# The low part of every weight computed on VectorE in place of GpSimd, in a two-block fp32 model

## The chip, the cores and the metric

The kernel runs on one core of a Trainium2 chip. The metric is the device time of one execution in microseconds. The kernel before takes 2074.5 us, the median of three runs (2071.7, 2074.5, 2074.66).

## The reference

512 tokens of width 1024 go through two blocks in float32. Weights lie in DRAM, 175 MB of loads in all.

- Block 1: `x + rmsnorm(m @ w_out)`, where `m` joins a causal attention (8 heads, low-rank queries and keys of rank 256, rotary positions) and a short gated convolution; then a gated FFN, `(silu(h @ w_gate) * (h @ w_up)) @ w_down` with 2816 hidden features, and an embedding gate, `x + sigmoid(x @ w_ple_gate) * rmsnorm(p @ w_ple_proj)`.
- Block 2, two layers: retention (4 heads, keys of 256, values of 512, decays by chunk) with a squared-ReLU MLP of 4096, and a chunk attention (16 heads of 64, relative bias) with another such MLP; then a last RMS norm.

```python
def rmsnorm(x, g):
    xf = x.astype(jnp.float32)
    y = xf * lax.rsqrt(jnp.mean(xf * xf, axis=-1, keepdims=True) + EPS)
    return (y * g.astype(jnp.float32)).astype(x.dtype)

def _sqrelu_mlp(h, w1, w2):
    u = jax.nn.relu(h @ w1)
    return (u * u) @ w2
```

## The kernel before, in words

**Data and products.** Features lie on the partitions: `x0` to `x7` are eight tiles of 128 features x 512 tokens. Every float32 product is made of three float32r matmuls (`mm3`, L147 to L150). For that each operand is split in a first part, the value rounded to float32r, and a second part, what the rounding left. For activations the two parts are a `pair`: `split` (L113) and `split_gain` (L118; ScalarE at L120, VectorE at L121) make it. For the weights they are the tiles `wh` and `wl`.

**Weights.** `load_weights` (L132) takes one block of up to 128 x 1024 weights (512 KB): a load on SP's queue into `wr`, a copy on ScalarE that rounds it into `wh` (through the helper at L111), and the subtraction `wl = wr - wh` on GpSimd (L137). It is called 354 times; 298 of the blocks are 1024 wide. `wr`, `wh` and `wl` have three buffers each. The instructions are put 80 places ahead of where they are written (`HW`), so that a block is split some weights before TensorE needs it.

**Order.** TensorE's order is the program's own (L79): generators pause after each 128-row part, and products that are independent are pulled in between before each step that waits for another engine. The orders of VectorE, ScalarE, GpSimd and SP are made by a scheduler from the program's order and the priorities (`HW`, `HC`, `HT`).

**Steps around the change.** A norm's `Norm.column` (L236) sums by transposes on TensorE (L240); its `root` (L244 to L259) is a chain of twelve small VectorE operations, from a reduction (L247) to L259; `spread` (L262) hands the result back to TensorE (L265), which waits for it. The heads of the attentions make scores (L311 to L333), `turn` (L335) transposes the probabilities (L340) and splits them into two parts (`pt`: a copy on ScalarE through L111, a subtraction on VectorE through L108), and `pv` (L347, L355) multiplies by the values. The embedding gate's `embed_add` (L854) and `Next.take` (L866) add to `x`, split the new `x` for the next products and square it for the next norm. VectorE's small helpers are `mul` (L102), `add` (L105) and `sub` (L108), so that their instructions carry these lines whoever calls them.

**GpSimd's other work.** It issues the load of the gains (L453), a store of the rotary table to DRAM (L500) and eight loads from there (L504), and runs two multiplications near the end (L952).

Of the kernel before, what the change touches and what calls it, by code (L numbers as in the profile page):

```python
# [21 lines left out]
# How many instructions ahead of their place the weights', the norms' and the embedding's are taken up,  # L22
# and how many parts of the filling products run before each step that waits for another engine.
HW = 80  # the weights' parts
N_E = (19, 11)  # embedding's norm: before its column, before its rows
W_OUT = (8, 2, 2, 13, 13)  # the first boundary
DOWN = (12, 1, 3, 10, 12)  # the second boundary
HC = 100  # roots and rows of the norms
HE = 60  # the embedding's products
HT = 30  # turned probabilities  # L30
PER = (14, 10, 6)  # the last heads of the first attention
OUT = (6, 6)  # the attention's norm
LAT = (6, 6, 12, 6, 5, 8, 2)  # before the first attention
HID = (0, 9)  # FFN's norm
N_RET = (8, 5)  # retention's norm
N_MLP = ((9, 8), (9, 5))  # the MLPs' norms
N_CH = (14, 12)  # chunk attention's norm
GG = (6, 7, 6)  # a retention head's products and norm
FIN = (5, 8)  # the final norm
CO = (4, 11)  # the convolution's norm  # L40
PER2 = (10,) * 8 + (13, 10, 9) + (10,) * 5 + (3,)  # the heads of the chunk attention
# [19 lines left out]
def kernel(  # L61
# [7 lines left out]
    nc = tc.nc  # L69
# [11 lines left out]
    # ---------------------------------------------------------------- tiles and single steps  # L81
# [12 lines left out]
    def f32(ap):  # L94
        return ap.bitcast(F32)
# [17 lines left out]
    def split(dst, src, rows=slice(0, P)):  # L113
        """src as the sum of two float32r parts, exactly."""
        copy(dst[rows, 0, :], src[rows, :])
        sub(dst[rows, 1, :], src[rows, :], f32(dst[rows, 0, :]))
# [15 lines left out]
    def load_weights(t, src, c):  # L132
        raw, hi, lo = t
        sp.dma_start(raw[:, c], src[:, c])
        with tc.high_priority(offset=HW):
            copy(hi[:, c], raw[:, c])
            nc.gpsimd.tensor_tensor(out=lo[:, c], in0=raw[:, c], in1=f32(hi[:, c]), op=ALU.subtract)  # L137
# [14 lines left out]
    # Products come as generators that pause after each 128-row part, so that others run in between; after  # L152
    # the last part it is their caller that pauses, once what reads the product is in place.
# [23 lines left out]
    def units4(outs, src, acts, prepare=None, loaded=None, tok=ALL, pool=None):  # L177
        """Four products at once, in the order of the rows that they share."""
        loaded = [] if loaded is None else loaded
        for kk in range(KT // 2):  # L180
            if kk == len(loaded):
                loaded += load4(src, 1, acts, prepare, kk, pool if kk < 3 else None)
            w = loaded[kk]
            for k in range(2):
                a = acts[2 * kk + k]
                for m in range(4):
                    c = slice(k * T + m * P, k * T + (m + 1) * P)
                    mm3(outs[m][:, tok], w[0][:, c], w[1][:, c], a[:, 0, tok], a[:, 1, tok],
                        kk + k == 0, kk == KT // 2 - 1 and k == 1)
                    yield  # L190

    def units_tok(outs, src, r0, acts):
        """Products with the tokens on the partitions."""
        nk = len(acts)
        for kk in range(nk // 2):
            w = weights(src[(r0 + kk) * P:(r0 + kk + 1) * P, :])
            for t in range(NT):
                ts = slice(t * P, (t + 1) * P)
                for k in range(2):
                    a = acts[2 * kk + k]  # L200
                    c = slice(k * T, (k + 1) * T)
                    mm3(outs[t], a[:, 0, ts], a[:, 1, ts], w[0][:, c], w[1][:, c],
                        kk + k == 0, 2 * kk + k == nk - 1)
                    if 2 * kk + k < nk - 1 or t < NT - 1:
                        yield
# [11 lines left out]
    class Norm:  # L217
        """1/sqrt(mean of squares + eps) over the features: a column per token tile, and along the rows."""
# [25 lines left out]
        def root(self, ps):  # L244
            """A guess from the exponent, a Newton step with the constants that suit it, and a cubic step."""
            a, na, u, h, y, w = (small(dt=d, tag=g)[:, :self.nt] for d, g in ((F32, "sm"),) * 4 + ((I32, "smi"), (F32, "sm")))
            dve.tensor_reduce(out=a, in_=ps.rearrange("p (t f) -> p t f", f=P)[:, :self.nt, :], op=ALU.add, axis=AX.X)  # L247
            dve.tensor_scalar(a, a, 1.0 / self.n, EPS, ALU.mult, ALU.add)
            dve.tensor_scalar(y, a.bitcast(I32), -0.5, 1595932665.0, ALU.mult, ALU.add)
            dve.tensor_scalar(na, a, -0.703952253, None, ALU.mult)  # L250
            y = y.bitcast(F32)
            mul(u, y, y)
            mul(u, u, na)
            dve.scalar_tensor_tensor(out=y, in0=u, scalar=0.703952253 * 2.38924456, in1=y, op0=ALU.add, op1=ALU.mult)
            mul(u, y, y)
            mul(h, u, a)
            dve.tensor_scalar(w, y, 0.375, None, ALU.mult)
            dve.scalar_tensor_tensor(out=h, in0=h, scalar=-10.0 / 3.0, in1=h, op0=ALU.add, op1=ALU.mult)
            dve.scalar_tensor_tensor(out=w, in0=h, scalar=5.0, in1=w, op0=ALU.add, op1=ALU.mult)  # L259
            self.col = w  # L260
# [13 lines left out]
        def then(self, f):  # L274
            """Run f once the rows are there."""
# [11 lines left out]
    class SplitNorm:  # L287
        """The same in two halves of the tokens, so that the first is done while the second is computed."""
# [11 lines left out]
    class Head:  # L300
        """One head of softmax attention; q and k feature-major, v token-major."""
# [9 lines left out]
        def scores(self, i):  # L311
# [4 lines left out]
            if self.stacked:  # L316
                # q's two parts on the two halves of the rows, against the first part of k in both
# [6 lines left out]
            # minus the scaled scores, and their least per row, which is minus the maximum  # L324
# [22 lines left out]
        def pv(self):  # L347
            """Rows 0-63 and 64-127 of the result add up to the head's output."""
# [14 lines left out]
    def value_tile(pool, ps, col=None):  # L363
        """Values of eight heads, the two parts of each head side by side."""
# [15 lines left out]
    def attention(n, head, fill, per, ptp, last):  # L380
        """The heads in a software pipeline; parts of `fill` run in between on the tensor engine."""
# [24 lines left out]
    # ---------------------------------------------------------------- loads that everything needs  # L406
# [5 lines left out]
    # the table of the first activations is loaded while the data is on its way  # L412
# [5 lines left out]
    # per-layer embedding: its projection does not need x, and fills in while norms are on their way  # L418
# [24 lines left out]
    # ---------------------------------------------------------------- first block: mixer  # L443
    ys, ys_t, mixed = [], [], []
    n_post = SplitNorm(D)
    with tc.tile_pool(name="m1", bufs=1) as m1, tc.tile_pool(name="pt1", bufs=1) as ptp:
# [25 lines left out]
        # the rotary angles as turns, reduced exactly: 16 frequencies times 8 spans of 64 tokens  # L472
        trig = m1.tile([P, T], F32, name="trig", tag="trig")

        def angles():
# [25 lines left out]
            # cos in 32 rows, then -sin and sin in 16 rows each, twice  # L501
# [7 lines left out]
        # keys of an even and an odd head: 64 features of the head, 64 of the rotated part, in turned order  # L509
# [122 lines left out]
        def conv_out():  # L632
            """The convolution's part of the output projection, its norm applied to the products."""
# [61 lines left out]
        # the attention's part of the output projection, its norm applied to the products  # L695
# [15 lines left out]
        def att_out():  # L711
# [4 lines left out]
            # the last three tiles in halves of the tokens  # L716
# [17 lines left out]
    def post_norm_add(norm, ys, gname, nxt):  # L734
        """x plus the normed ys on the norm's tokens, and the next operand's parts, tile by tile."""
# [7 lines left out]
    def boundary(norm, ys, gname, nxt, fill, counts, src, acts, loaded):  # L743
        """From the last product of one step to the first four of the next, in halves of the tokens."""
# [16 lines left out]
    # ---------------------------------------------------------------- first block: FFN  # L761
# [98 lines left out]
    class Next:  # L860
        """Parts of x times the next pre-norm's gain, and its sum of squares."""
# [25 lines left out]
    # ---------------------------------------------------------------- the other block's MLP  # L887
# [40 lines left out]
    def finish(hid, ws):  # L928
        """The last three tiles in halves of the tokens, and the final norm of each half."""
# [44 lines left out]
    # ---------------------------------------------------------------- retention  # L974
    with tc.tile_pool(name="m2", bufs=1, reuse_waits="tile") as m2:
# [37 lines left out]
        def values(h):  # L1013
            """Token-major values, centred over the head's features: the outputs then have mean zero."""
# [101 lines left out]
    # ---------------------------------------------------------------- chunk attention  # L1116
# [93 lines left out]
def _constants():  # L1210
    """Arrays that depend on the shapes alone."""
# [115 lines left out]
```

## Time and profile before

| | us |
|---|---|
| median of three runs | 2074.5 |
| span of the profiled execution | 2072.2 |
| TensorE busy (matmuls) | 2001.0 |
| VectorE busy | 1121.0 |
| GpSimd busy | 821.0 |
| ScalarE busy | 804.2 |

The profiled execution has no time of its own beside its span; the median of the runs lies 2.3 us above that span. In the rows below PE is TensorE, DVE is VectorE, ACT is ScalarE, POOL is GpSimd. A busy time is a sum of the durations of an engine's instructions; it contains what an instruction stood still after it had begun.

### The profile page before, as it was taken

How to read it: one execution, taken by the hardware profiler on the slowest of the kernel's cores; microseconds unless marked ns; L12 is line 12 of the kernel's file. 1: busy time of each engine (PE TensorE's matmuls, PEld its weight loads, DVE VectorE, ACT ScalarE, POOL GpSimd, SP SyncE). 2: the span in 40 equal slices, each digit the busy share in tenths (PEclk: the TensorE clock that was granted, in tenths of full speed). 3: DMA queues.
4: the chain of work that ended last, by engine and by line, in shares of the span. 5: the costliest groups of instructions: out<-in, count | busy, mean ns of one | idle time of the engine just before them, and what ended most of it. 6: DMA issues, size and time to landing. Idle time of an engine off the chain costs nothing.

```text
span 2072.2 us, 23982 instructions
## 1 busy us (share of the span) xinstructions
PE 2001.0 (97%) x9340; PEld 1649.8 (80%) x9340; DVE 1121.0 (54%) x1813; ACT 804.2 (39%) x1298; POOL 821.0 (40%) x370
## 2 busy tenths in 40 slices
PE   7899799999998899999999999999999999999998
PEld 5777688888887688888878888888877777888887
DVE  7877883042348844605466253346587876243255
ACT  4577452232233443314433222223466653222222
POOL 5323424444452333343334444444322234444442
PEclk9999999999999999999999999999999999999999
DMA  4112213232332223232223323232222223232332
GB/s 165 59 62 73 96 56 100 93 101 93 99 97 94 72 77 97 82 100 74 82 92 92 102 92 102 92 102 91 97 82 68 64 78 101 92 102 92 102 92 71
DMA packets 58786, 185.32 MB, mean 89 GB/s; under 512 B 6784, under 2 KB 10000, under 8 KB 58672
## 3 DMA queue, kind: packets, MB, share of 16 engines
q1 hardware_dynamic: 53648, 175.76, 26.7%
q10 hardware_dynamic: 4688, 7.60, 1.3%
q8 instruction: 73, 1.20, 0.2%
q0 software_dynamic: 336, 0.42, 0.1%
q14 instruction: 41, 0.34, 0.1%
HBM read 181.56 MB, written 2.20 MB: 89 GB/s over the span
## 4 chain that ended last, share of the span: by engine, by line
PE 45%; issue 25%; POOL 16%; DVE 9%; ACT 3%; DMA 1%; POOLq 0%; SPq 0%; ACTq 0%; DVEq 0%
POOL wl L137 16%; PE bank L148 14%; PE bank L150 14%; PE bank L149 14%; DVE pair L108 1%; DVE tmp L102 1%; DVE small L102 1%; DVE tmp L105 1%; PE bank L355 1%; DVE x L105 1%; DVE pair L121 1%; PE bank L320 1%; DVE pair L105 0%; DVE pt L108 0%; DVE pair L126 0%
## 5 line engine op out<-in xcount | busy, mean ns | idle before, releaser
L137 POOL TENSOR_TENSOR wl<-wr,wh 128x1024 fp32r<-128x1024 f32 (+4 forms) x354 | 813.9, 2301 | 1213.5 <-ACT wh L111 1213.0
L148 PE MATMUL bank<-pair,wh 128*128 128x512 f32 (+1 forms) x2550 | 985.0, 386 | 11.8 <-ACT pair L120 8.1
L150 PE MATMUL bank<-pair,wh 128*128 128x512 f32 (+1 forms) x2550 | 972.9, 382 | 12.8 <-DVE pair L121 9.1
L149 PE MATMUL bank<-pair,wl 128*128 128x512 f32 (+1 forms) x2550 | 971.8, 381 | 1.9 <-POOL wl L137 1.9
L111 ACT ACTIVATE wh<-wr 128x1024 fp32r<-128x1024 f32 (+4 forms) x354 | 352.7, 998 | 888.1 <-PE bank L150 576.6
L150 PEld LDWEIGHTS bank<-pair,wh 128*128 128x128 f32 x2550 | 481.6, 189 | 110.7 <-DVE pair L121 13.9
L148 PEld LDWEIGHTS bank<-pair,wh 128*128 128x128 f32 x2550 | 481.8, 189 | 104.0 <-ACT pair L120 9.4
L149 PEld LDWEIGHTS bank<-pair,wl 128*128 128x128 f32 x2550 | 482.3, 189 | 89.2 <-POOL wl L137 3.2
L108 DVE TENSOR_TENSOR pair<-tmp,pair 128x512 fp32r<-128x512 f32 (+1 forms) x156 | 232.0, 1489 | 73.3 <-ACT pair L111 72.2
L102 DVE TENSOR_TENSOR tmp<-bank,rb 128x512 f32<-128x512 f32 (+1 forms) x140 | 94.4, 678 | 258.4 <-PE bank L150 249.8
L105 DVE TENSOR_TENSOR x<-x,bank 128x512 f32<-128x512 f32 (+1 forms) x99 | 66.3, 671 | 267.6 <-PE bank L150 267.5
L111 ACT ACTIVATE pair<-tmp 128x512 fp32r<-128x512 f32 (+1 forms) x188 | 118.4, 630 | 115.9 <-DVE tmp L1076 34.3
L105 DVE TENSOR_TENSOR tmp<-tmp 128x512 f32<-128x512 f32 (+1 forms) x107 | 90.9, 850 | 50.4 <-ACT tmp L233 48.7
L121 DVE SCALAR_TENSOR_TENSOR pair<-x,gn,pair 128x512 fp32r<-128x512 f32 (+1 forms) x56 | 69.8, 1248 | 25.6 <-ACT pair L120 25.5
L148 PE MATMUL bank<-wh,pair 128*128 128x512 f32 x200 | 79.7, 399 | 0.0
L150 PE MATMUL bank<-wl,pair 128*128 128x512 f32 x200 | 77.9, 390 | 0.0
L149 PE MATMUL bank<-wh,pair 128*128 128x512 f32 x200 | 77.9, 390 | 0.0
L327 ACT ACTIVATE tmp<-tmp,small 128x512 f32<-128x512 f32 (+1 forms) x96 | 53.2, 555 | 37.9 <-DVE small L325 35.5
L108 DVE TENSOR_TENSOR pt<-bank,pt 128x512 fp32r<-128x512 f32 (+1 forms) x96 | 42.9, 485 | 21.5 <-ACT pt L111 21.1
L120 ACT ACTIVATE pair<-x,gn 128x512 fp32r<-128x512 f32 (+1 forms) x56 | 36.5, 654 | 33.3 <-DVE x L105 32.8
L894 DVE SCALAR_TENSOR_TENSOR tmp<-tmp 128x512 f32<-128x512 f32 x64 | 46.8, 733 | 2.1
L111 ACT ACTIVATE pt<-bank 128x512 fp32r<-128x512 f32 (+1 forms) x96 | 38.0, 434 | 19.3 <-PE bank L340 17.8
(150 smaller groups left out, 1351.0 us busy)
## 6 DMA issues: line engine op xcount, KB each, us to landing
wr<-in_m_w_dram SPq DMA_DIRECT2D x128, 512.0 KB, 3.7
wr<-in_r_qkg_dram SPq DMA_DIRECT2D x32, 512.0 KB, 3.5
wr<-in_w_gate_dram SPq DMA_DIRECT2D x20, 512.0 KB, 3.4
wr<-in_w_up_dram SPq DMA_DIRECT2D x20, 512.0 KB, 3.4
wr<-in_w_down_dram SPq DMA_DIRECT2D x16, 512.0 KB, 3.5
wr<-in_r_v_dram SPq DMA_DIRECT2D x16, 512.0 KB, 3.4
wr<-in_r_out_dram SPq DMA_DIRECT2D x16, 512.0 KB, 3.7
wr<-in_a_qk_dram SPq DMA_DIRECT2D x16, 512.0 KB, 3.4
```

What stands on the lines that cost most here:

```text
L102: dve.tensor_tensor(out=out, in0=a, in1=b, op=ALU.mult)
L105: dve.tensor_tensor(out=out, in0=a, in1=b, op=ALU.add)
L108: dve.tensor_tensor(out=out, in0=a, in1=b, op=ALU.subtract)
L111: act.activation(out, a, AF.Copy)
L120: act.activation(dst[:, 0, tok], src[:, tok], AF.Copy, scale=gain)
L121: dve.scalar_tensor_tensor(out=dst[:, 1, tok], in0=src[:, tok], scalar=gain, in1=f32(dst[:, 0, tok]), op0=ALU.mult, op1=ALU.subtract)
L137: nc.gpsimd.tensor_tensor(out=lo[:, c], in0=raw[:, c], in1=f32(hi[:, c]), op=ALU.subtract)
L148: pe.matmul(out, lhsT=ah, rhs=bh, start=start, stop=False)
L149: pe.matmul(out, lhsT=al, rhs=bh, start=False, stop=False)
L150: pe.matmul(out, lhsT=ah, rhs=bl, start=False, stop=stop)
L327: act.activation(s[:, :n], s[:, :n], AF.Exp, bias=self.mx[:, col], scale=-1.0, accum_out=self.sm[:, col])
L894: dve.scalar_tensor_tensor(out=t, in0=t, scalar=0.0, in1=t, op0=ALU.max, op1=ALU.mult)
```

## The change

The subtraction that makes the low part of a block of weights is issued on VectorE, through the helper `sub`, in place of GpSimd. Its operands, its priority and the number of subtractions stay.

```diff
@@ -134,7 +134,7 @@
         sp.dma_start(raw[:, c], src[:, c])
         with tc.high_priority(offset=HW):
             copy(hi[:, c], raw[:, c])
-            nc.gpsimd.tensor_tensor(out=lo[:, c], in0=raw[:, c], in1=f32(hi[:, c]), op=ALU.subtract)
+            sub(lo[:, c], raw[:, c], f32(hi[:, c]))
```

The helper that it calls, in both kernels:

```python
    def sub(out, a, b):
        dve.tensor_tensor(out=out, in0=a, in1=b, op=ALU.subtract)
```

All other lines of the diff take out comments and doc strings. TensorE's and SP's orders are the same in both kernels. The 354 rows are gone from GpSimd's order, whose eight loads of L504 now follow each other, and stand in VectorE's, where the scheduler has put them as follows. ScalarE's `wh` copies have moved a little against its other work.

VectorE at the root of the attention's group norm, before (`att0` to `att3` are the attention's result, `small` the columns of the root, `wl` the low part of a weight):

```order
L247 TENSOR_REDUCE small_2010<-bank_2005 128x4
L121 SCALAR_TENSOR_TENSOR pair_2041<-att2_648,gn_77,pair_2041 128x512
L248 TENSOR_SCALAR small_2010<-small_2010 128x4
L102 TENSOR_TENSOR pair_1983<-bank_1998,rb_1894 128x512
L249 TENSOR_SCALAR small_2014<-small_2010 128x4
L250 TENSOR_SCALAR small_2011<-small_2010 128x4
L121 SCALAR_TENSOR_TENSOR pair_2044<-att3_649,gn_77,pair_2044 128x512
L102 TENSOR_TENSOR small_2012<-small_2014 128x4
L102 TENSOR_TENSOR small_2012<-small_2012,small_2011 128x4
L254 SCALAR_TENSOR_TENSOR small_2014<-small_2012,small_2014 128x4
```

The same place now, from the second small product on:

```order
L102 TENSOR_TENSOR small_2012<-small_2014 128x4
L108 TENSOR_TENSOR wl_2143<-wr_2141,wh_2142 128x1024
L102 TENSOR_TENSOR small_2012<-small_2012,small_2011 128x4
L108 TENSOR_TENSOR wl_2321<-wr_2319,wh_2320 128x512
L254 SCALAR_TENSOR_TENSOR small_2014<-small_2012,small_2014 128x4
L108 TENSOR_TENSOR wl_2321<-wr_2319,wh_2320 128x512
L102 TENSOR_TENSOR small_2012<-small_2014 128x4
```

Three weight rows now stand inside the root, which had none.

VectorE where the embedding gate ends and retention's norm begins, now (`x6` and `x7` are the last tiles of the activations, `tmp_5473` the sum of squares, `small_5711` the column of retention's root):

```order
L102 TENSOR_TENSOR tmp_5649<-tmp_5649,pair_5048 128x512
L121 SCALAR_TENSOR_TENSOR pair_5653<-x6_84,gn_77,pair_5653 128x512
L105 TENSOR_TENSOR x7_85<-x7_85,tmp_5649 128x512
L105 TENSOR_TENSOR tmp_5473<-tmp_5473,tmp_5656 128x512
L108 TENSOR_TENSOR wl_5786<-wr_5784,wh_5785 128x1024
L121 SCALAR_TENSOR_TENSOR pair_5659<-x7_85,gn_77,pair_5659 128x512
L105 TENSOR_TENSOR tmp_5473<-tmp_5473,tmp_5662 128x512
L247 TENSOR_REDUCE small_5711<-bank_5706 128x4
L108 TENSOR_TENSOR wl_5817<-wr_5815,wh_5816 128x1024
L248 TENSOR_SCALAR small_5711<-small_5711 128x4
```

Before, the same rows stood there without the two `wl`, and the addition to `x7` stood one place earlier, ahead of the split of `x6`.

VectorE in a head of the chunk attention, now (`pt` is the second part of the turned probabilities, `kl` the second part of a later head's keys):

```order
L1135 SCALAR_TENSOR_TENSOR tmp_11504<-bank_11414,rb_11134 128x512
L108 TENSOR_TENSOR wl_11729<-wr_11727,wh_11728 128x1024
L108 TENSOR_TENSOR pt_11528<-bank_11529,pt_11527 128x4x128
L108 TENSOR_TENSOR kl_11511<-tmp_11504,pair_11506 64x512
L108 TENSOR_TENSOR pt_11528<-bank_11539,pt_11527 128x3x128
L108 TENSOR_TENSOR pt_11528<-bank_11548,pt_11527 128x2x128
L108 TENSOR_TENSOR pt_11528<-bank_11553,pt_11527 128x128
```

A weight row stands right ahead of the first `pt` row; before, the two rows of `kl` stood before and after that row and no weight's.

## Rows read from the trace of the kernel before

**Rows 1.** The page, part 1: busy time, share of the span, instructions.

```profile
PE 2001.0 (97%) x9340; PEld 1649.8 (80%) x9340; DVE 1121.0 (54%) x1813; ACT 804.2 (39%) x1298; POOL 821.0 (40%) x370
```

**Rows 2.** Waits of TensorE: what it waited for, us in total, times, longest.

```profile
PE bank L265 <- DVE small L259: 25.1, 8, 6.5
PE bank L150 <- DVE pair L121: 9.1, 6, 2.6
PE bank L148 <- ACT pair L120: 8.1, 4, 6.2
PE bank L355 <- DVE pt L108: 4.7, 5, 2.2
...
PE bank L150 <- DVE pair L108: 3.7, 2, 1.9
...
PE bank L149 <- POOL wl L137: 1.9, 3, 1.3
```

**Rows 3.** Busy time by stretch: length, then engine by engine, clock, DMA share, GB/s.

```profile
41.00:51.00 10.00, 3.51 (x13) 2.81 (x12) 7.99 (x11) 1.23 (x2) 6.25 (x7) 0.66 0.40 120
...
310.00:600.00 290.00, 290.00 (x1280) 239.90 (x1279) 82.85 (x83) 81.72 (x100) 129.95 (x55) 1.00 0.30 95
...
665.00:712.00 47.00, 40.76 (x166) 31.36 (x165) 43.51 (x57) 19.78 (x30) 17.79 (x7) 0.89 0.23 76
...
1480.00:1680.00 200.00, 200.00 (x928) 150.67 (x927) 157.60 (x393) 128.77 (x286) 51.68 (x25) 1.00 0.23 71
```

**Rows 4.** Groups of instructions by form: busy us, mean ns, idle before them.

```profile
L137 POOL TENSOR_TENSOR wl<-wr,wh 128x1024 fp32r<-128x1024 f32 x298 | 728.7, 2446 | 1089.1 <-ACT wh L111 1088.9
...
L108 DVE TENSOR_TENSOR pair<-tmp,pair 128x512 fp32r<-128x512 f32 x140 | 213.1, 1524 | 70.3 <-ACT pair L111 69.6
...
L121 DVE SCALAR_TENSOR_TENSOR pair<-x,gn,pair 128x512 fp32r<-128x512 f32 x40 | 62.2, 1556 | 25.5 <-ACT pair L120 25.5
```

**Rows 5.** Timeline of VectorE, the embedding gate's end: start and duration, us.

```profile
677.33 0.69 DVE L102 TENSOR_TENSOR tmp<-tmp,pair 128x512 f32<-128x512 f32 x1
678.05 2.78 DVE L105 TENSOR_TENSOR x<-x,tmp 128x512 f32<-128x512 f32 x1
```

**Rows 6.** Timeline of GpSimd, the same stretch.

```profile
677.45 2.83 POOL L137 TENSOR_TENSOR wl<-wr,wh 128x1024 fp32r<-128x1024 f32 x1 [6.76 <-ACT wh L111]
```

**Rows 7.** The page, part 5: all subtractions of the weights.

```profile
L137 POOL TENSOR_TENSOR wl<-wr,wh 128x1024 fp32r<-128x1024 f32 (+4 forms) x354 | 813.9, 2301 | 1213.5 <-ACT wh L111 1213.0
```

**Rows 8.** Timeline of VectorE at a root beside which GpSimd is idle.

```profile
655.88 0.43 DVE L108 TENSOR_TENSOR pair<-x,pair 128x256 fp32r<-128x256 f32 x1 [0.48 <-ACT pair L111]
656.56 0.69 DVE L247 TENSOR_REDUCE small<-bank 128x4 f32<-128x512 f32 x1 [0.25 <-PE bank L240]
...
658.88 0.16 DVE L259 SCALAR_TENSOR_TENSOR small<-small 128x4 f32<-128x4 f32 x1
```

**Rows 9.** Timeline of VectorE at the first norm's root.

```profile
36.56 0.69 DVE L247 TENSOR_REDUCE small<-bank 128x4 f32<-128x512 f32 x1 [2.01 <-PE bank L240]
...
38.65 3.91 DVE L102 TENSOR_TENSOR small<-small 128x4 f32<-128x4 f32 x2
...
42.79 4.49 DVE L102 TENSOR_TENSOR small<-small 128x4 f32<-128x4 f32 x2
...
47.52 0.16 DVE L259 SCALAR_TENSOR_TENSOR small<-small 128x4 f32<-128x4 f32 x1
```

**Rows 10.** Timeline of GpSimd at the first norm's root.

```profile
38.34 1.61 POOL L504 DMA_DIRECT2D trig<-hbm  x3
39.96 2.38 POOL L137 TENSOR_TENSOR wl<-wr,wh 128x1024 fp32r<-128x1024 f32 x1
42.28 2.62 POOL L504 DMA_DIRECT2D trig<-hbm  x5
44.90 2.35 POOL L137 TENSOR_TENSOR wl<-wr,wh 128x1024 fp32r<-128x1024 f32 x1
```

**Rows 11.** Tile `pt` from 1480 to 1690 us: who waited for it (us, times).

```profile
  DVE pt L108: 16.2, 21
```

## The prediction

> **What bounds the kernel now.** I read the busy times first. TensorE is busy for 97% of the span, VectorE for 54%, GpSimd for 40% [rows 1]. The sum of the products is not touched, so the change can only reach the 71 us in which TensorE stands still, and the stretches in which it runs at its lower clock level.
>
> The second view is the list of what TensorE waits for [rows 2]. VectorE ends most of these waits: 25.1 us behind the roots of the norms (eight waits, the longest 6.5), then 9.1 and 3.7 us behind the second parts of activations (`pair`), 4.7 us behind turned probabilities (`pt`). ScalarE's 8.1 us are 6.2 us at the very start, where the first input is on its way, and 1.9 us of the same splits. GpSimd itself, which makes the second parts of the weights (`wl`), is waited for only three times, 1.9 us together. So the price of GpSimd is not its lateness.
>
> The third view, busy times by stretch [rows 3], says where there is nothing to gain: in the FFN (310 to 600 us) TensorE is busy for 290.00 of 290 us and in the chunk attention (1480 to 1680) for 200.00 of 200. It also shows the clock: a mean grant of 0.66 from 41 to 51 us and 0.89 from 665 to 712 us. [...]
>
> What GpSimd does cost is in the durations of VectorE. The `pair` subtraction over 512 columns takes 1.52 us in the mean of 140, the scaled split 1.56 us in the mean of 40 [rows 4]. An undisturbed row of 512 takes 0.69 us [rows 5]. The next row, which starts at 678.05, takes 2.78 us [rows 5], while GpSimd runs a `wl` from 677.45 for 2.83 us [rows 6]: VectorE is held until GpSimd is done, 2.09 us longer than its own work. [...]
>
> **The change part by part.** *Removed*: 354 GpSimd subtractions, 813.9 us [rows 7]; 298 of them are 1024 wide at 2.45 us [rows 4]. With them go the holds.
>
> *Added*: the same 354 on VectorE. No two-input row of 1024 stands in the trace. 512 columns take 0.69 us [rows 5], 256 take 0.43 us [rows 8], so 256 more cost 0.26 and 1024 cost 0.69 + 2 x 0.26 = 1.21 us; the upper end is two rows of 512, 1.38. I take 1.21. Scaled from GpSimd's total (1.21/2.446 = 0.495) that is 403 us for all. The two groups of [rows 4] give back 140 x (1.52 - 0.69) + 40 x (1.56 - 0.69) = 151 us, and other forms were held too. VectorE ends at 1121 + 403 - 151 = 1373 us or less, at most 66%. A hold of 2.09 us thus becomes 1.21 us in the queue where a `wl` stands in the same place (-0.88, 42%), and nothing where it stands elsewhere.
>
> *The first norm's root.* Alone the root takes from 656.56 to 659.04, 2.48 us [rows 8]. At the start it runs from 36.56 to 47.68 [rows 9], with two pairs of tiny products lasting 3.91 and 4.49 us while GpSimd subtracts at 39.96 and 44.90 and issues table loads at 38.34 and 42.28 [rows 10]. TensorE stands still for it for 6.5 us [rows 2], so from about 41.2. The new order has one `wl` ahead of the root and none in it: it would end near 39.0, or 40.3 behind that `wl`, before TensorE is there. But the eight table loads (1.61 + 2.62 us) stay on GpSimd, now in one row. The product at 38.65 stood still for 1.3 us before the subtraction of 39.96 began, under those loads. If all eight hold, the root ends near 43.2 and 2.0 us of the wait are left; if none does, 0. I take 1.5 left, nearer to the row that was held: **-5.0**. [...]
>
> *The clock behind it.* 10 us at 0.66 are 3.4 us lost. With the idle time mostly gone I take half back: **-1.7**. The 47 x 0.11 = 5.2 us of the other stretch I leave, as TensorE will still stand still there.
>
> *The other roots.* 25.1 - 6.5 = 18.6 us in seven waits. The last one comes after the last weight and stays; the one in the second boundary keeps three `wl` rows in its way. The other five lose 0.88 each: **-4.4**. In the attention's norm the new order puts a whole and two half `wl` into the root, against the holds of before.
>
> *Splits.* 9.1 + 3.7 + 1.9 = 14.7 us. The chain before retention is typical: VectorE is busy for 43.5 of 47 us there [rows 3], and the holds are all that makes it late; the new order has a `wl` between most of its splits. Between 42% (each hold replaced on the spot) and 100% I take two thirds: **-9.8**.
>
> *Turned probabilities.* Of 4.7 us a quarter: **-1.2**.
>
> *Costs.* In both attentions a `wl` now stands just ahead of `pt` subtractions, right ahead of the first in ten of the 16 chunk heads. What covers it: VectorE waited there anyway for ScalarE's copy, 16.2 us in 21 waits [rows 11], 0.77 each; 1.21 - 0.77 = 0.44 is uncovered. For 16 heads that is 7.0 us at most, for ten 4.4; TensorE had no wait there and so some reserve: **+3.0** (0 to 7.0). For the first attention's eight heads 3.5 at most, I take half: **+1.7**. Without any cover each `wl` costs its 1.21.
>
> *Steady products: 0.* From 310 to 600 us, 55 `wl` add 55 x 1.21 = 67 us to VectorE's 83 of 290 [rows 3], so it is half idle still; a `wl` is made two weights ahead. TensorE's order and the loads' order don't change.
>
> Sum: -5.0 - 1.7 - 4.4 - 9.8 - 1.2 + 3.0 + 1.7 = -17.4 us on a span of 2072.2, so 2054.8. The median of the runs, 2074.5, is 2.3 above that span; I predict 2074.5 - 17.4 = **2057.1 us**, with 2047 to 2067 for this case.
>
> **The rivals.**
> *Given back.* Each `wl` lands in VectorE's queue in the very place where its hold was, and waits there for ScalarE's first part (`wh`), with all that stands behind it. For it: the order's many `wl` rows between splits. Against it: 2.09 against 1.21 us. Result 2070 to 2079, likeliest 2074.5.
>
> *Slower: VectorE too full in the attentions.* Each of 24 heads has a `wl` ahead of its `pt` row or its softmax. From 1480 to 1680 us VectorE is already busy for 157.6 of 200 us; 51.68 x 0.495 = 26 us of `wl` make up to 184, 92% [rows 3]. If no idle time covers them and TensorE waits the full 1.21 per head, that is +29.0 in place of the two costs above, against -22.1 of gains: +6.9, **2081.4 us**. It decides from 22.1/24 = 0.92 us per head. Against it: part of the 157.6 is holds that go. [...]
>
> *Larger gain.* All of these waits go (25.1 + 9.1 + 4.7 + 3.7 + 1.9 = 44.5) and both low stretches of the clock (8.6): 2074.5 - 53.1 = 2021.4. Against it: a root's own 2.48 us and ScalarE's rows remain.
>
> *Not what it says.* GpSimd's subtractions remain: the new order has none of them, so 1 in 100, 2074.5.
>
> **How the numbers follow.** The forecast has 0.58, the larger gain 0.05, given back 0.14, slower 0.22, not what it says 0.01. With 0.2% of 2074.5, 4.1 us, as about what a measurement can tell from no change, faster has 0.58 + 0.05 = 0.63, same 0.15, slower 0.22. The range: downward the forecast with the first root free (-1.5), all of the splits (-4.9), all of the clock (-6.9) and no costs (-4.7), 2057.1 - 18.0 = 2039; upward to the slower rival, 2081. About half of that rival's chance and most of the larger gain's lie outside.
>
> **What would show it.** GpSimd's busy time falls below 15 us; `wl` rows on VectorE take 1.2 us; `pair` subtractions fall to 0.7 us and the scaled split to 0.75; VectorE's busy time lies between 1200 and 1373 us; TensorE's wait at 41 us falls to 2 us or less; the chunk attention shows at most 0.2 us of new waits per head. I am wrong if TensorE waits for `wl` on VectorE by more than 10 us in all, if new waits of `pt` over 1 us per head appear between 1480 and 1680 us, if the stretch from 310 to 600 us is no longer full, or if the wait at 41 us stays with GpSimd free of subtractions.

## The result and the profile after

The changed kernel takes 2029.2 us (median of four runs, 2028.2 to 2030.7) against 2074.6: the ratio is 0.9776, with a 95% interval of 0.9762 to 0.979, so 45 us faster. The forecast was 17.4 us faster, 2057.1 us; the direction was right, and the size 2.6 times too small. The time lies below the range of 2047 to 2067, and below the 2039 to which the prediction's best cases add up. The span went from 2072.2 to 2028.9 us, by 43.3. Three executions of the later experiments ran in a slow state (2209.6 us at `HW` 60, 2837.3 at `HW` 100, 4999.9 of the kernel before beside them) and are left out of the medians below.

The page of the changed kernel, part 1, against [rows 1]:

```profile
PE 1991.5 (98%) x9340; PEld 1647.9 (81%) x9340; DVE 1197.2 (59%) x2167; ACT 805.5 (40%) x1298; POOL 7.1 (0%) x16
```

TensorE runs the same 9340 matmuls in 9.5 us less. VectorE took over 354 rows, 405.7 us of work, and is busy for only 76 us more: its other rows got some 330 us shorter.

What TensorE waits for now (us in total, times, longest), against [rows 2]:

```profile
PE bank L148 <- ACT pair L120: 9.5, 4, 6.1
PE bank L265 <- DVE small L259: 9.1, 6, 2.3
PE bank L340 <- ACT tmp L331: 4.5, 4, 2.5
PE bank L240 <- DVE tmp L105: 4.1, 3, 2.3
PE bank L150 <- DVE pair L121: 1.5, 3, 0.9
PE bank L355 <- ACT pt L111: 0.9, 1, 0.9
PE bank L355 <- DVE pt L108: 0.8, 1, 0.8
PE bank L148 <- ACT tmp L111: 0.3, 1, 0.3
```

The waits for the roots fell from 25.1 to 9.1 us. Those for VectorE's splits (L150) fell from 12.8 to 1.5, while those for ScalarE's splits (L120) rose from 1.9 to 3.4 beside the 6.1 of the start. No matmul waits for a weight's low part. All idle time of TensorE between matmuls adds up to 64.9 us before and 30.8 after.

The groups by form (busy us, mean ns, idle before them), against [rows 4]:

```profile
L108 DVE TENSOR_TENSOR wl<-wr,wh 128x1024 fp32r<-128x1024 f32 x298 | 364.1, 1222 | 144.6 <-ACT wh L111 143.7
...
L108 DVE TENSOR_TENSOR pair<-tmp,pair 128x512 fp32r<-128x512 f32 x140 | 95.7, 686 | 11.2 <-ACT pair L111 10.8
...
L121 DVE SCALAR_TENSOR_TENSOR pair<-x,gn,pair 128x512 fp32r<-128x512 f32 x40 | 29.8, 745 | 1.9 <-ACT pair L120 1.7
```

A weight's row takes 1.22 us on VectorE where GpSimd needed 2.45. The `pair` subtraction is back from 1524 to 686 ns, the scaled split from 1556 to 745.

The first norm's root, VectorE's timeline, against [rows 9]:

```profile
36.80 0.36 DVE L102 TENSOR_TENSOR small<-small 128x4 f32<-128x4 f32 x2
37.20 0.16 DVE L254 SCALAR_TENSOR_TENSOR small<-small 128x4 f32<-128x4 f32 x1
37.39 0.36 DVE L102 TENSOR_TENSOR small<-small 128x4 f32<-128x4 f32 x2
...
37.98 0.16 DVE L259 SCALAR_TENSOR_TENSOR small<-small 128x4 f32<-128x4 f32 x1
```

And GpSimd's timeline beside it, against [rows 10]:

```profile
37.21 4.21 POOL L504 DMA_DIRECT2D trig<-hbm  x8 [2.46 <-DMA hbm<-sc]
```

The second pair of products runs in 0.36 us in the middle of the eight table loads, where a pair took 3.91 and 4.49 before. The root is done at 38.1 us, and TensorE does not wait for it at all.

The trace of the kernel before already had the two products of its second pair apart, in narrower windows of VectorE's timeline:

```profile
42.79 0.16 DVE L102 TENSOR_TENSOR small<-small 128x4 f32<-128x4 f32 x1
```

```profile
42.99 4.29 DVE L102 TENSOR_TENSOR small<-small 128x4 f32<-128x4 f32 x1
```

The first of them ran free under the five table loads of [rows 10] (42.28 to 44.90 us). The second ended at 47.28 us, when the subtraction beside it ended (47.25).

Two stretches, the FFN and the chunk attention, at their new times (length, then PE, PEld, DVE, ACT, POOL, clock, DMA share, GB/s), against [rows 3]:

```profile
282.00:572.00 290.00, 290.00 (x1281) 240.11 (x1281) 118.57 (x138) 81.77 (x100) 0.00 (x0) 1.00 0.30 95
...
1439.00:1639.00 200.00, 200.00 (x928) 150.70 (x927) 159.65 (x417) 128.53 (x286) 0.00 (x0) 1.00 0.22 69
```

Both stay full. In the chunk attention VectorE has 24 rows more than before and is busy for 159.65 in place of 157.60 us: the holds that went paid for the weights' rows that came.

**Where the time came from.** TensorE's order is the same in every kernel here, so the start of one and the same matmul can be compared between two traces. The table gives how much earlier (-) or later a matmul starts than in the kernel before, at places named by their time there; each number is the difference of two start times. The columns after the first are the experiments below. Each column is one execution; that of e4_twice was 5.8 us slower than the median of its runs, the others lie within 3.1 us of theirs.

| place, us | changed | e1_both | e5_memset | e3_waits | e3_steady | e4_twice | e6_first |
|---|---|---|---|---|---|---|---|
| 47.8 | -8.3 | +1.8 | -8.4 | -8.3 | +0.2 | -7.4 | -9.6 |
| 310 | -27.7 | +34.3 | -26.0 | -27.6 | +0.5 | -1.2 | -10.6 |
| 600 | -28.0 | +34.0 | -26.2 | -27.9 | +0.5 | -1.5 | -10.6 |
| 712 | -37.8 | +49.4 | -38.7 | -39.9 | +0.3 | -0.2 | -10.5 |
| 1045 | -37.9 | +50.3 | -38.7 | -39.9 | +0.3 | -0.2 | -10.5 |
| 1062 | -41.3 | +53.6 | -42.2 | -43.4 | -1.3 | -2.0 | -10.5 |
| 1480 | -41.4 | +53.7 | -42.3 | -43.4 | -1.4 | -2.0 | -10.5 |
| 1680 | -41.4 | +58.4 | -42.3 | -43.5 | -1.4 | +8.4 | -10.5 |
| 1720 | -43.1 | +65.9 | -44.9 | -45.2 | -1.6 | +12.1 | -10.4 |
| end | -43.3 | +65.6 | -45.1 | -45.1 | -2.0 | +11.3 | -10.5 |

The first column moves in four places only: up to 310 us (27.7 of the 43.3), and at the boundaries near 650, 1050 and 1700 us. From 310 to 600, 712 to 1045, 1062 to 1680 and 1720 on it moves by 0.3 us or less.

### The profile page after: what moved, and what is told of

Its sections match the earlier page's. It is cut to its first block, busy times and chain, and to the rows that moved or that the text cites. A ratio compares the mean times of both kernels' runs of the same rounds, so it can differ in the third digit from the quotient of the medians.

```text
span 2028.9 us, 23868 instructions
## 1 busy us (share of the span) xinstructions
PE 1991.5 (98%) x9340; PEld 1647.9 (81%) x9340; DVE 1197.2 (59%) x2167; ACT 805.5 (40%) x1298; POOL 7.1 (0%) x16
## 4 chain that ended last, share of the span: by engine, by line
PE 90%; DVE 5%; ACT 3%; issue 1%; DMA 0%; POOL 0%; POOLq 0%; DVEq 0%; ACTq 0%
PE bank L148 29%; PE bank L150 28%; PE bank L149 28%; PE bank L355 1%; DVE wl L108 1%; PE bank L320 1%; PE bank L340 1%; PE bank L319 1%; DVE tmp L105 1%; DVE pair L108 1%; ACT tmp L327 1%; ACT wh L111 1%; PE bank L265 0%; DVE pair L121 0%; DVE x L105 0%
## 5 line engine op out<-in xcount | busy, mean ns | idle before, releaser
L148 PE MATMUL bank<-pair,wh 128*128 128x512 f32 (+1 forms) x2550 | 983.3, 386 | 9.5 <-ACT pair L120 9.5
L150 PE MATMUL bank<-pair,wh 128*128 128x512 f32 (+1 forms) x2550 | 971.9, 381 | 1.7 <-DVE pair L121 1.5
L148 PEld LDWEIGHTS bank<-pair,wh 128*128 128x128 f32 x2550 | 481.6, 189 | 101.2 <-ACT pair L120 10.8
L150 PEld LDWEIGHTS bank<-pair,wh 128*128 128x128 f32 x2550 | 481.3, 189 | 96.8 <-DVE pair L121 3.8
L108 DVE TENSOR_TENSOR wl<-wr,wh 128x1024 fp32r<-128x1024 f32 (+4 forms) x354 | 405.5, 1146 | 153.6 <-ACT wh L111 152.3
L108 DVE TENSOR_TENSOR pair<-tmp,pair 128x512 fp32r<-128x512 f32 (+1 forms) x156 | 106.7, 686 | 11.7 <-ACT pair L111 10.8
L105 DVE TENSOR_TENSOR tmp<-tmp 128x512 f32<-128x512 f32 (+1 forms) x107 | 68.1, 640 | 36.7 <-ACT tmp L233 36.0
L148 PE MATMUL bank<-wh,pair 128*128 128x512 f32 x200 | 79.7, 398 | 0.3 <-ACT tmp L111 0.3
L150 PE MATMUL bank<-wl,pair 128*128 128x512 f32 x200 | 78.0, 390 | 0.0
L108 DVE TENSOR_TENSOR pt<-bank,pt 128x512 fp32r<-128x512 f32 (+1 forms) x96 | 43.5, 486 | 15.5 <-ACT pt L111 15.1
L148 PEld LDWEIGHTS bank<-wh,pair 128*128 128x128 f32 x200 | 37.6, 188 | 8.6 <-ACT tmp L111 0.7
L150 PEld LDWEIGHTS bank<-wl,pair 128*128 128x128 f32 x200 | 37.5, 188 | 8.0
```

Source lines behind the costliest of these rows:

```text
L105: dve.tensor_tensor(out=out, in0=a, in1=b, op=ALU.add)
L108: dve.tensor_tensor(out=out, in0=a, in1=b, op=ALU.subtract)
L148: pe.matmul(out, lhsT=ah, rhs=bh, start=start, stop=False)
L150: pe.matmul(out, lhsT=ah, rhs=bl, start=False, stop=stop)
```

## The experiments

Two theories stood against each other. *Hold*: rows of VectorE no longer stand still while GpSimd reads. *Lateness or order*: the low part is ready sooner, or the scheduler's new orders are better. All times are medians of three to ten executions in three rounds, against the kernel before on the same chip (whose medians were 2074.5 to 2076.2 us).

**e1_both and e5_memset: is it GpSimd's reading?** Both keep VectorE's subtraction; GpSimd then writes over the raw weight, once with a subtraction, once with zeros. The two kernels have the same orders on all other engines; only GpSimd's instruction differs. Against the changed kernel, 18 places in VectorE's order and 4 in ScalarE's differ. The computed low parts are unchanged. In the code below, against the changed kernel, `sub(...)` stands for the call that is kept.

```diff
-            sub(lo[:, c], raw[:, c], f32(hi[:, c]))
+            sub(...); nc.gpsimd.tensor_tensor(out=raw[:, c], in0=raw[:, c], in1=f32(hi[:, c]), op=ALU.subtract)   # e1
+            sub(...); nc.gpsimd.memset(raw[:, c], 0.0)   # e5
```

> VectorE makes every low part as in the changed kernel, and GpSimd then subtracts over the same block once more, in place in the raw weight, whose value nobody reads. Theory 'hold' (the gain came from rows of VectorE no longer standing still while GpSimd reads): the holds are back on top of the queue's 405 us, the pair subtraction over 512 columns has a mean over 1.2 us, VectorE is busy for over 1400 us, and the time is 2060 to 2110 us. Theory 'lateness or order' (the gain came from the low part being ready sooner, 1.22 in place of 2.45 us, or from the scheduler's new orders): both are kept, so 2029 us, within 8.

> As e1_both with the same orders, but GpSimd fills the raw weight with zeros after use in place of the subtraction, so that it writes SBUF and reads nothing. Theory 'hold, reads only' (a row of VectorE with two SBUF inputs stands still only against a GpSimd instruction that reads): the pair subtraction stays at 0.69 to 0.75 us in the mean, and the time is within 6 us of 2029; only one-input rows of VectorE could be held. Theory 'hold, any GpSimd instruction': the pair subtraction is over 0.9 us, and the time is above 2040 us.

e1_both takes 2136.4 us (ratio 1.0289, 1.0271 to 1.0307), above the 2060 to 2110 that "hold" gave, and e5_memset 2029.9 us (0.9775, 0.976 to 0.979). In e1_both, waits and groups:

```profile
PE bank L265 <- DVE small L259: 37.6, 10, 9.0
...
PE bank L149 <- DVE wl L108: 2.8, 4, 1.3
```

```profile
L137 POOL TENSOR_TENSOR wr<-wr,wh 128x1024 f32<-128x1024 f32 x298 | 771.8, 2590 | 1110.9 <-DVE wl L108 983.1 <-ACT tmp L327 31.2 <-issue 23.6
...
L108 DVE TENSOR_TENSOR pair<-tmp,pair 128x512 fp32r<-128x512 f32 x140 | 114.4, 819 | 11.7 <-ACT pair L111 10.8
```

The roots' waits are back and larger, though VectorE makes the low part: by the traces it is done 1.26 us behind its `wh` in the median, as in the changed kernel, where GpSimd needed 2.47 before. TensorE waits for it only 2.8 us. So lateness is not the cause. (Part 4 of the page before puts 16% of the chain that ended last on GpSimd's subtractions. TensorE waited 1.9 us for them, so that share is no price either.) The `pair` mean is 0.82 us and not over 1.2 as expected: GpSimd's copy of the work now starts behind VectorE's (983.1 of its 1110.9 us of idle time end there) and meets other rows, by the waits the roots above all. In e5_memset, groups by form:

```profile
L137 POOL MEMSET wr<- 128x1024 f32 x298 | 284.9, 956 | 1512.7 <-DVE wl L108 1399.6 <-DVE small L329 38.2 <-DVE small L102 19.5
L108 DVE TENSOR_TENSOR pair<-tmp,pair 128x512 fp32r<-128x512 f32 x140 | 95.9, 686 | 11.2 <-ACT pair L111 10.8
```

354 GpSimd instructions that only write cost nothing that the time shows, and rows with two SBUF inputs keep their 686 ns. That a fill is shorter than a subtraction is not the reason: by the trace 89 of these 140 rows ran beside a fill, and none took over 694 ns. One-input rows are another matter. The same line in e5_memset and then in the changed kernel (a one-input operation of the root; ns as least, median and longest):

```profile
L249 DVE TENSOR_SCALAR small<-small x21: 159/170/970, 36.5 to 2018.3; 128x4 int32<-128x4 int32 x15, 128x2 int32<-128x2 int32 x6
```

```profile
L249 DVE TENSOR_SCALAR small<-small x21: 156/169/172, 36.6 to 2020.1; 128x4 int32<-128x4 int32 x15, 128x2 int32<-128x2 int32 x6
```

Four of them took 333 to 970 ns, each beside a fill, in place of 172 at most. So in these runs GpSimd's subtractions, which read, held the two-input rows (`pair` 1524 ns in the mean before, 819 in e1_both) and its fills, which only write, did not (686); some one-input rows were held by both (L249 2378 ns at most in e1_both, 970 in e5_memset). Why the two kinds of row differ, the profile does not show.

**e3_waits and e3_steady: which weights matter?** The low parts of 116 blocks around the waits go to VectorE and the other 238 to GpSimd, and the other way round. The line takes the place of the `sub` of the changed kernel; dots stand for arguments.

```diff
+            NL.append(1); n = len(NL) - 1; (sub(...)) if any(n in r for r in (range(54), range(98, 130), range(176, 185), range(280, 297), range(350, 354))) else nc.gpsimd.tensor_tensor(...)   # e3_waits; e3_steady: not any(...)
```

> VectorE makes the low parts of 116 blocks (the first 54, and 32, 9, 17 and 4 around the later boundaries), GpSimd those of the 238 blocks that are split in the steady stretches and the chunk attention. Theory 'hold, and only where TensorE waits': the whole gain is kept, 2026 to 2034 us, with VectorE's pair subtraction still slow in the steady stretches. Theory 'relief over the whole span': a gain in proportion to the blocks, 45 x 116/354 = 15, so 2060 us.

> The other way round: VectorE makes the 238 low parts of the steady stretches, GpSimd the 116 around the boundaries. Theory 'hold, and only where TensorE waits': no gain, 2068 to 2078 us. Theory 'relief over the whole span': 45 x 238/354 = 30 us less, 2044 us.

e3_waits takes 2029.1 us (0.9772, 0.9757 to 0.9787), e3_steady 2074.3 us (0.9991, 0.998 to 1.0003). A third of the blocks carries the whole gain, the other two thirds none. e3_waits, groups by form:

```profile
L137 POOL TENSOR_TENSOR wl<-wr,wh 128x1024 fp32r<-128x1024 f32 x232 | 566.6, 2442 | 1325.2 <-ACT wh L111 1325.2
L108 DVE TENSOR_TENSOR pair<-tmp,pair 128x512 fp32r<-128x512 f32 x140 | 207.0, 1480 | 64.5 <-ACT pair L111 64.0
```

The `pair` subtraction is as slow as before, 1480 ns, and the time is that of the changed kernel. The row on which I priced the hold, in its mean over the span, is mostly from places where a hold is free.

**e6_first: the first norm's root alone.** Only the first 12 blocks go to VectorE (`if n < 12`).

> Only the first 12 blocks' low parts on VectorE, all others on GpSimd: the first norm's root alone. Theory 'hold by the subtractions only' (the table loads hold nothing): the wait of 6.5 us goes wholly, and with it the low clock behind it, 8 to 10 us less, 2065 to 2067 us, and no wait over 0.5 us between 35 and 50 us. The forecast's terms (1.5 us of the wait left under the table loads, half of the clock returned): 6.7 us less, 2068 us, with a wait of 1 to 2 us there.

It takes 2064.5 us, 10.0 us less than before (0.9948, 0.9933 to 0.9962). Its waits for roots:

```profile
PE bank L265 <- DVE small L259: 18.6, 7, 4.5
```

The one of 6.5 us is gone from the 25.1, the other seven stand. The table's column is -10.6 at 310 us, of which 2.2 were there by 35 us (the two waits for splits at 19 and 23 us, 1.6 together, are gone) and 7.4 came between 35 and 47.8 us. TensorE has no wait left between 35 and 50 us, as "hold by the subtractions only" said, where the forecast's terms had 1 to 2 us. The eight table loads stand on GpSimd as before and hold nothing.

**e2_halves: a shorter hold.** GpSimd keeps all blocks, each split into two instructions; the code is set against the kernel before and written out as a loop, and `m` is the middle of the block.

```diff
-            nc.gpsimd.tensor_tensor(out=lo[:, c], in0=raw[:, c], in1=f32(hi[:, c]), op=ALU.subtract)
+            for h in (slice(c.start, m), slice(m, c.stop)):
+                nc.gpsimd.tensor_tensor(out=lo[:, h], in0=raw[:, h], in1=f32(hi[:, h]), op=ALU.subtract)
```

> The kernel before with each GpSimd subtraction cut into two of half the width. Theory 'hold for the length of one GpSimd instruction': a row of VectorE waits for 1.4 us at most in place of 2.4 and gets in between the halves; the pair subtraction's mean falls from 1.52 to 1.1 to 1.3 us and the time to 2050 to 2070 us. Theory 'lateness': two halves take 2.86 us in place of 2.45, so every low part is later, 2075 to 2085 us.

It takes 2062.5 us (0.9936, 0.992 to 0.9953). Groups by form:

```profile
L137 POOL TENSOR_TENSOR wl<-wr,wh 128x512 fp32r<-128x512 f32 x596 | 837.7, 1427 | 970.1 <-ACT wh L111 969.9
...
L108 DVE TENSOR_TENSOR pair<-tmp,pair 128x512 fp32r<-128x512 f32 x140 | 130.5, 935 | 70.4 <-ACT pair L111 69.9
```

GpSimd works longer in all (944 us busy against 821), a low part is ready later (2.63 us behind its `wh` in the median against 2.47), and the kernel is 12 us faster. The `pair` mean of 0.94 us is below the 1.1 to 1.3 expected, and the longest such row took 1.79 us in place of 2.90, as if a row of VectorE waits for one GpSimd instruction and gets in before the next. This too is against lateness.

**e4_twice: what a place in VectorE's queue costs.** The changed kernel with the subtraction issued twice; the scheduler moves other rows around the longer work.

> The changed kernel with each low part computed twice on VectorE, which adds 354 rows and 405 us of VectorE's time (1197 to about 1600 us, 79%); the scheduler moves other rows around them. It prices a place in VectorE's queue. Theory 'the queue has room' (a weight's row costs nothing in the steady stretches and in the chunk attention, and little elsewhere): 2029 to 2041 us, with TensorE full from 310 to 600 and in the chunk attention. Theory 'each row in the way costs its length', as in the forecast's two cost terms (0.44 and more per head in 24 heads, and as much around the boundaries): 116 blocks around the waits x 1.2 x one third = 46, so 2060 to 2090 us, with new waits of the chunk attention of 10 us and more.

It takes 2079.5 us (against before 1.0025, 1.0013 to 1.0037), 50 us above the changed kernel for 354 more rows. The FFN and the two MLPs stay full; from 1480 to 1680 us the table shows +10.5. The new wait there, beside a mean granted clock of 0.98 from 1498 to 1688 us of this run (1.00 in the changed kernel's chunk attention):

```profile
PE bank L340 <- DVE tmp L333: 5.0, 8, 1.0
```

So both theories were half right. The first row of each block finds room in the chunk attention, the second does not; around the boundaries the second takes back most of what the change had gained. The experiment does not tell the rows' length from the moved orders.

**Weights' rows placed otherwise.** In the changed kernel, `HC` 200 and `HT` 60; `HW` 40, 60 and 100 in place of 80.

> The changed kernel with the norms' roots and rows taken up 200 places ahead in place of 100 and the turned probabilities 60 in place of 30, which moves weights' rows behind some pt rows and out of one root in the first attention. Theory 'what is left are weights' rows in the way': 3 to 6 us less, 2023 to 2026 us. Theory 'what is left are the chains' own lengths': 2027 to 2031 us.

> The changed kernel with the weights' parts taken up 40 instructions ahead in place of 80, so that their rows on VectorE stand later against the chains of the boundaries. Theory 'what is left are weights' rows in the way': 2020 to 2027 us. Theory 'the place no longer matters': 2027 to 2031 us. Should a weight's part come too late, TensorE would wait for it on VectorE, 2035 us and more.

> As h_hw40 with 60. Weights' rows in the way: 2023 to 2028 us. The place no longer matters: 2027 to 2031 us.

> As h_hw40 with 100, so earlier. Weights' rows in the way: 2031 to 2036 us, since more of them stand ahead of the chains. The place no longer matters: 2027 to 2031 us.

They take 2033.2 (0.9795, 0.978 to 0.981), 2027.6 (0.9764, 0.9746 to 0.9781), 2026.4 (0.9759, 0.9741 to 0.9776) and 2024.6 us (0.9753, 0.9736 to 0.977); the last three differ by less than their intervals, on both sides of 80. Moving the roots and `pt` ahead made it no faster: 2033.2 lies above the ranges of both theories (2023 to 2026, 2027 to 2031). `HW` 100 lies below both of its ranges (2031 to 2036, 2027 to 2031), so weights' rows that stand earlier were not in the way. All intervals of `HW` overlap that of the change, so none is shown to beat it: where the rows stand matters little once the holds are gone.

## Why the prediction was wrong in size

The mechanism was right, and so was the price of the moved rows: 1.22 us for one (1.21 forecast), 405.7 us for all (403), no GpSimd time to speak of, full steady stretches. What the holds had cost was priced too low. Over the span VectorE's other rows gave back some 330 us; the prediction had counted 151 in two groups and named no sum for the rest. VectorE's 1197.2 us of busy time lie just under the 1200 to 1373 announced. The terms of the sum were mis-sized. Against [rows 2], and with these rows of the kernel before that the sum left out:

```profile
PE bank L240 <- DVE tmp L105: 3.8, 4, 1.5
...
PE bank L148 <- DVE tmp L102: 2.0, 1, 2.0
...
PE bank L355 <- ACT pt L111: 1.7, 1, 1.7
PE bank L148 <- ACT pair L111: 1.7, 1, 1.7
PE bank L340 <- ACT tmp L331: 1.6, 2, 1.4
PE bank L149 <- DVE pair L108: 1.2, 1, 1.2
```

| term | forecast | measured | from |
|---|---|---|---|
| first norm's root | -5.0 | -6.5 | its wait is gone |
| clock | -1.7 | -9.5 | TensorE busy 2001.0 to 1991.5 |
| other roots | -4.4 | -9.5 | 18.6 to 9.1 |
| splits | -9.8 | -9.8 | 14.7 to 1.5 + 3.4 (9.5 less the start's 6.1) |
| turned probabilities | -1.2 | -3.9 | 4.7 to 0.8 |
| chunk attention | +3.0 | 0.0 | 1480 to 1680 in the table |
| first attention | +1.7 | +2.9 | L340, 1.6 to 4.5 (behind scores, not `pt`) |
| waits left out | 0 | -7.0 | 2.0 + 1.7 + 1.2 + 1.9 (GpSimd) + 0.8 (L355) - 0.3 (L240) - 0.3 (new, L148) |

The measured column sums to -43.3, the change of the span.

- *The clock* is the largest miss. I took half of one stretch and left the other, since "TensorE will still stand still there". There were more than these two. Two others of the trace of the kernel before, which I left out:

```profile
177.00:184.00 7.00, 5.42 (x19) 4.81 (x20) 6.52 (x15) 6.53 (x12) 1.01 (x1) 0.52 0.26 77
1045.00:1062.00 17.00, 15.35 (x60) 11.88 (x59) 12.18 (x11) 6.38 (x9) 7.27 (x3) 0.90 0.20 64
```

Both went wholly, as did the one from 41 to 51 us; that from 665 to 712 us shrank from 10.2 to 6.8 us at a granted clock of 0.50. Over the span the mean grant was 0.990 before and is 0.995 now:

```profile
core 0: 2072.2 us, clock 0.990
```

```profile
core 0: 2028.9 us, clock 0.995
```

That is 0.010 x 2072 = 20.7 us lost before and 0.005 x 2029 = 10.1 after, 10.6 apart, and TensorE's busy time shows 9.5 of it. Ahead of the last norm the granted clock stood at 0.50 in six stretches, 34.1 us together, and in three now, 13.7 us; each began in a wait of TensorE or within 2 us of its end. In the first of the six, matmuls over 512 columns start 0.43 us apart (from 49.07 us), and 0.23 once the clock is back at 1.00 (from 50.93). The clock went up where the waits went.
- *"A hold of 2.09 us thus becomes 1.21 us in the queue"* failed for the roots (18.6 to 9.1 where I had 18.6 to 14.2). In the root of the attention's norm, three weights' rows stand inside the chain as the order said:

```profile
199.07 1.22 DVE L108 TENSOR_TENSOR wl<-wr,wh 128x1024 fp32r<-128x1024 f32 x1
...
200.28 0.68 DVE L108 TENSOR_TENSOR wl<-wr,wh 128x512 fp32r<-128x512 f32 x1
...
200.96 0.68 DVE L108 TENSOR_TENSOR wl<-wr,wh 128x512 fp32r<-128x512 f32 x1
```

Even so, the root takes 6.0 us from its reduction to its end in place of 8.3, and TensorE's wait there fell from 3.1 to 1.1. GpSimd had held this root for one long run of three subtractions (5.07 us); I had priced a single hold of 2.09. The root of the second boundary, which I left at its wait of 4.5 us since three `wl` rows stand in its way, fell to 2.3 too. The largest share came from the root at 291 us: its last step but one had stood for 2.31 us beside a subtraction, and its wait of 3.2 us is gone wholly, where I had taken off 0.88.
- *"If all eight hold"*: the table loads hold nothing, as e6_first (no wait left between 35 and 50 us) and the timeline after (a pair of products in 0.36 us under them) show. The term came out at -6.5, and the row at 38.65 misled me. That row is two products, the first of 3.71 us; like the long one of the second pair, it ended 0.03 us behind a subtraction. Why these two stood still for 1.3 and 1.9 us before the subtraction's span begins stays open.
- *The costs in the attentions* were taken from the idle time of VectorE before. They left out that its own rows there would get shorter: busy for 157.6 us before and 159.65 after, with the weights' rows in it. By the trace a weight's row stands right ahead of the first `pt` row in eight of the 16 heads, not ten, and no matmul waited there. In the first attention the new wait is one of 2.5 us at 173.6 us, for ScalarE's last step on the scores (L331) and not for `pt`.
- *Turned probabilities* lost 3.9 of their 4.7 us, where I had given back a quarter. The prediction has no rows for that quarter.
- *The waits left out* were small ones on VectorE, on ScalarE and on GpSimd's low parts, 7.0 us together. That a hold stood behind each of them is likely and not shown one by one.
- *Splits* came out at their -9.8 in part by luck: VectorE's waits went by 88% and not by two thirds, and ScalarE's rose.

The rivals: "given back" and "slower" did not come; e4_twice shows where the latter lies, at a second 1.22 us per block. "Larger gain" (2021.4, given 0.05) came nearest, 7.8 us off where the forecast was 27.9 off. It named the right places, waits and low clock; the roots' own 2.3 us and ScalarE's rows remained, as said against it, and part of the measured gain came from waits and stretches of low clock that it did not list.

## What to carry to other kernels

Where GpSimd and VectorE both read SBUF, as here (`pair` rows of 1524 ns in the mean beside GpSimd's subtractions and of 686 beside its fills), price GpSimd's instructions by what they do to VectorE's chains in the stretches in which the bounding engine waits, and not by their own lateness or by VectorE's busy share over the span. Two thirds of the blocks could have stayed where they were; the third around the boundaries held the gain. When a forecast takes waits away, take away the low clock that the trace shows behind them as well: it was a fifth of this gain (9.5 of 43.3).

## What the runs showed that I had not expected

- GpSimd's subtraction beside VectorE's, whose result nobody reads, made the kernel 61 us slower than the kernel before, and 107 us slower than the changed kernel.
- Cutting GpSimd's instruction in two won 12 us, though GpSimd was busy for 123 us more.
- A second 1.22 us per block on VectorE cost 50 us, with TensorE's share of busy time at 97% and VectorE's at 75%: the first was paid for by the holds that went, and nothing paid for the second.
